# Retention projection of a hybrid diffusion layer: read-back rows in buffers of their own, and the first two output blocks taken by halves of the tokens

## The chip, the cores and the metric

The kernel runs on one core of one Trainium2 chip. The metric is device time in microseconds (us) of one execution; lower is better. The median of three runs of the kernel before is 1781.46 us (1779.99 to 1782.4).

## The reference

The kernel computes one transformer-like layer on 1024 latent tokens and 256 context tokens with 1024 channels, in float32. The part that matters here is the end of its first half:

```python
o_ret = _merge_heads(on) * jax.nn.silu(g)                      # gated retention, tokens x 1024
merged = sigmoid(gate_na) * (o_na @ w_proj_na) + sigmoid(gate_ret) * (o_ret @ w_proj_ret)
x = x + g1 * (merged @ w_out)
hx2 = modulate(rmsnorm(x, norm2_g), sh2, sc2)
x = x + g2 * conv_ffn(hx2, w_up, conv_w, conv_b, w_down)
```

`o_ret @ w_proj_ret` is the product of this case: 1024 tokens by 1024 channels by 1024 channels.

## The kernel before

Everything is held with channels on the 128 partitions and tokens along the free dimension. 1024 tokens are two halves of 512, 1024 channels are eight blocks of 128. A float32 operand is used as a pair: `split` makes a high part by a cast on ScalarE (ACT, line 86) and a low part by a subtraction on VectorE (DVE, line 87). A product is then three matmuls on TensorE (PE): high times high, high times low, low times high (lines 110, 111, 112). Each takes a 128x128 piece of weights and 512 tokens.

Weights arrive by `wload`: `rawload` (lines 89 to 92) brings 128x512 floats (256 KB) into a ring of three places (tag `raw`), and `split` turns them into a pair in a ring of six places (tag `wc`). All DMAs are issued by SyncE (SP) in one fixed order; an SP instruction that waits holds up all that stand behind it. The order on every engine is set at build time by a list scheduler from the order in which the code is written; `late` keeps an instruction at its place in the program's order.

The stages around the change, one after the other on PE:

1. **Gates.** Twelve-matmul steps of a seven-product scheme (`Gates`, rows `u` at L1374). Each step splits one weight pair. Units of the retention store their results, the gated retention rows, to DRAM (`d_orr`: eight channel blocks `k`, each 1024 tokens). Units of the merge, the last ones, store to `d_pn` and `d_gate` (rows `c` at L1482).
2. **Retention projection** (`pr`, lines 110 to 112). For each of eight output blocks `db` and each half of the tokens a chain of 24 matmuls: eight channel blocks `k`, three matmuls each, against the eight row pairs `orr[half, k]`. The first weights tile of a block serves `k` 0 to 3, the second 4 to 7. Then DVE multiplies the sum by its gate (`sg`, L1595), GpSimd (POOL) adds the other branch (L1596), and `split` makes `mh` and `ml`.
3. **Output projection** (`om`, lines 121 to 123), whose weights are `w_out`, with the second norm, and then the feed-forward half.

Before stage 2 the sixteen half rows `orr[half, k]` are read back from `d_orr` by `orr_raw`, which uses `rawload`, so the ring of three that the weights use. Those of half 0 are loaded during the last ten gate steps, one a step; those of half 1 in the loop at `db == 0`. The pairs `orr` lie where the normalised input `hx` lay: rows of half 1 with `k` 4 to 7 take the places that the very last gate step still reads.

Of the kernel before, what the change touches and what calls it, by code (L numbers as in the profile page):

```python
# [8 lines left out]
F32 = mybir.dt.float32  # L9
F32R = mybir.dt.float32r  # L10
AF = mybir.ActivationFunctionType
ALU = mybir.AluOpType
# [4 lines left out]
P = 128  # L17
D = 1024
KB = D // P
# [10 lines left out]
RH = 4  # L30
# [10 lines left out]
def tile_hybrid_layer(ctx, tc: tile.TileContext, io, dbg=None):  # L41
    nc = tc.nc
    vec, act, pool, pe, sync = nc.vector, nc.scalar, nc.gpsimd, nc.tensor, nc.sync

    def sb(name, side, bufs=1):
        return tc.alloc_tile_pool(name=name, bufs=bufs, side=side, reuse_waits="tile")
# [11 lines left out]
    d_orr = dram.tile([RH * 2, P, T], F32, name="d_orr")  # L58
# [24 lines left out]
    wpool = sb("wstream", "left")  # L83

    def split(hi, lo, src, lo_eng=None):
        act.copy(hi, src)  # L86
        (lo_eng or vec).tensor_tensor(lo, src, hi.bitcast(F32), ALU.subtract)  # L87

    def rawload(src, pin=lambda ins: ins):
        raw = wpool.tile([P, 512], F32, tag="raw", bufs=3, name="raw")  # L90
        pin(sync.dma_start(raw, src))
        return raw

    def wtile():
        return wpool.tile([P, 2, 512], F32R, tag="wc", bufs=6, name="wc")

    def wload(src, lo_eng=None, into=None):
        raw = rawload(src)
        wc = into if into is not None else wtile()
        split(wc[:, 0], wc[:, 1], raw, lo_eng)  # L100
        return wc

    def chain(out, wcs, hi, lo, step=24):
        n = 4 * len(wcs)
        for k in range(n):
            wc = wcs[k // 4]
            c0 = (k % 4) * P
            wh, wl = wc[:, 0, c0 : c0 + P], wc[:, 1, c0 : c0 + P]
            xh, xl = hi(k), lo(k)
            pe.matmul(out, wh, xh, start=k == 0, stop=False)  # L110
            pe.matmul(out, wh, xl, start=False, stop=False)  # L111
            pe.matmul(out, wl, xh, start=False, stop=k == n - 1)  # L112
            if (k + 1) % step == 0 and k + 1 < n:
                yield

    def mm_a(out, wcs, hi, lo):
        for _ in chain(out, wcs, hi, lo):
            pass
# [415 lines left out]
    late = tc.keep_in_program_order  # L534
# [703 lines left out]
    def down_sums(pool_, j0, j1, bufs=8):  # L1238
        def load(j, n):
            t = pool_.tile([P, 512], F32, tag="pj", bufs=bufs, name="pj")  # L1240
            sync.dma_start(t, io["w_down"][n % 2, NH * (n // 2) + j])
            return t

        ts, store = [load(j0, n) for n in range(4)], None
        yield
        for j in range(j0, j1):
            nxt = []
            for n, (c, x, y, o) in enumerate(((1, 1, 0, 0), (3, 3, 1, 1), (2, 3, 0, 3), (4, 2, 3, 2))):
                late(pool.tensor_tensor(ts[o], ts[x], ts[y], ALU.subtract))
                if store:  # L1250
                    sync.dma_start(*store)
                store = (d_w[j, c - 1], ts[o])
                if j + 1 < j1:
                    nxt.append(load(j + 1, n))
                yield
            ts = nxt
        sync.dma_start(*store)
# [71 lines left out]
    KH = KB // 2  # L1329

    def g_ps(name):
        return pg.tile([P, 512], F32, tag="g", bufs=6, name=name)

    def g_raw(name):
        return rr.tile([P, 512], F32, tag="r", bufs=10, name=name)
# [21 lines left out]
    for n in range(KB):  # L1357
        raw = g_raw("onr")
# [128 lines left out]
    for db in range(KB):  # L1487
# [3 lines left out]
        wp = [wload(io["w_pna"][db, 0])]  # L1491
        for half in range(2):
            sl_ = slice(half * 512, half * 512 + 512)
            m = g_ps("pn")
            mm_a(m, wp, lambda k: ona[0][:, k, sl_], lambda k: ona[1][:, k, sl_])
            t = onap.tile([P, 512], F32, tag="pn", bufs=3, name="pnt")
            if (db, 0) in spilled:
                g = onap.tile([P, 512], F32, tag="sg", bufs=2, name="sgt")
# [24 lines left out]

    orr = {}

    def orr_raw(half, k):
        i, kb = (k // KH if half else 1 - k // KH), k % KH + KH * half
        orr[half, k] = [hxpool.tile([P, 512], F32R, tag=f"{t}{i}{kb}", bufs=1, name="orr") for t in ("high", "low")]
        return orr[half, k], rawload(d_orr[k, :, half * 512 : half * 512 + 512], late)

    gate_sums = down_sums(gr, RET_SUMS, GATE_SUMS)
    steps = interleaved(0, len(gu))
    n0, fetched = steps.index((len(gu) - 1, 0)), None
    for n, (i, k) in enumerate(steps):
        gu[i].step(k)
        if n % 3 == 1:
            next(gate_sums, None)
        if fetched:
            split(*fetched[0], fetched[1])
            fetched = None  # L1540
        if n0 <= n < n0 + 2 * RH:
            fetched = orr_raw(0, n - n0)
    wp0 = [wload(io["w_pret"][0, i]) for i in range(2)]
    for _ in gate_sums:
        pass
    gr.release()
# [6 lines left out]
    def gtile(half, dt, name):  # L1553
        return gpool[half].tile([P, 512], dt, tag="g", bufs=2 * KB + 1, name=name)

    sg = {}

    def merge_load(db, halves=(0, 1)):
        for half in halves:
            sg[db, 0, half] = gtile(half, F32, "sg")  # L1560
            sync.dma_start(sg[db, 0, half], d_pn[db, half])
            sg[db, 1, half] = t = gtile(half, F32, "sg")
            sync.dma_start(t, d_gate[2 * db + 1, half])
            if (db, 1) in spilled:
                act.activation(t, t, AF.Sigmoid)
# [4 lines left out]
    def brow(i, t):  # L1570
        sync.dma_start(t, d_ada[8 * i : 8 * i + 8].rearrange("a b -> (a b)").unsqueeze(0).to_broadcast([P, D]))
        return t

    pjp = sb("out_sums", "right")
    out_sums = down_sums(pjp, GATE_SUMS, NH, 7)
    mg = {}
    wp_next = wp0
    for db in range(KB):
        wp = wp_next
        if db == 0:  # L1580
            merge_load(0, (0,))
            for k in range(2 * RH):
                hl, raw = orr_raw(1, k)
                split(*hl, raw)
            merge_load(0, (1,))
        if db + 1 < KB:
            wp_next = [wload(io["w_pret"][db + 1, i]) for i in range(2)]
            merge_load(db + 1)
        if db == 2:
            brow(0, gate1)  # L1590
        for half in range(2):
            m = g_ps("pr")
            mm_a(m, wp, lambda k: orr[half, k][0], lambda k: orr[half, k][1])
            g = sg[db, 1, half]
            vec.tensor_tensor(g, m, g, ALU.mult)  # L1595
            (vec if db == KB - 1 else pool).tensor_tensor(g, g, sg[db, 0, half], ALU.add)  # L1596
            h_, l_ = gtile(half, F32R, "mh"), gtile(half, F32R, "ml")
            split(h_, l_, g)
            mg[db, half] = (h_, l_)
            if db > 1:  # L1600
                next(out_sums, None)
    pjp.release()
    wo = {}
    for kb in range(KB):
# [450 lines left out]
def build(nc, arrays):  # L2055
    io = {k: nc.dram_tensor(f"in_{k}", a.shape, mybir.dt.from_np(a.dtype), kind="ExternalInput").ap() for k, a in arrays.items()}
    io["out"] = nc.dram_tensor("out_0_dram", (T, D), F32, kind="ExternalOutput").ap()
    with tile.TileContext(nc) as tc:
        tile_hybrid_layer(tc, io)
# [11 lines left out]
```

## Time and profile before

| | before |
|---|---|
| median of three runs | 1781.46 us (1779.99 to 1782.4) |
| the profiled execution | 1783.34 us, span 1781.6 us |
| PE busy | 1728.4 us, 97% of the span |
| DVE, ACT, POOL busy | 73%, 48%, 32% |
| mean granted clock of PE | 0.988 |
| gates stage ends, retention projection begins to end | 929.0, 931.3 to 1027.6 us |

Times inside the span are us from its start. PE is busy nearly all the time, so a change of the time has to come from stretches in which PE waits or runs at a lower granted clock. A matmul row shows 0.39 us, but matmuls overlap: at full pace one starts every 0.227 us.

### The profile page before, as it was taken

What the parts mean: (1) busy time and instruction counts of PE and PEld (TensorE: products, weight loads), DVE (VectorE), ACT (ScalarE), POOL (GpSimd) and SP (SyncE); (2) the same over time, 40 slices, a digit from 0 to 9 for tenths busy, and PEclk for the clock granted to TensorE, in tenths of its full rate; (3) what the DMA queues carried; (4) which work ended last, traced back from release to release, by engine and by line L of the source; (5) the groups of instructions that cost most, each with busy time, mean ns of one, the idle gap of its engine ahead of it and who ended that gap; (6) DMA issues with size and microseconds to landing.
All of it is one profiled execution on the core that took longest, in us unless ns stands there. A gap on an engine that the chain in (4) does not pass through costs nothing.

```text
span 1781.6 us, 24740 instructions
## 1 busy us (share of the span) xinstructions
PE 1728.4 (97%) x8357; PEld 1431.6 (80%) x8357; DVE 1309.0 (73%) x2458; ACT 850.2 (48%) x1833; POOL 569.1 (32%) x477
## 2 busy tenths in 40 slices
PE   8799999999999999999999999989999999999997
PEld 3588888888888888778877888868888888788886
DVE  5878888765776766777655556879989989875755
ACT  5667666652443434443444333544444444554444
POOL 2610000002334343554412400065555555211444
PEclk9899999999999999999999999999999999999999
DMA  9133334432231212677558633642332332586754
GB/s 344 57 116 119 113 111 137 140 112 101 70 107 48 72 39 71 205 234 252 177 178 277 224 140 138 238 137 89 107 101 89 108 118 101 165 285 195 241 160 160
DMA packets 139552, 261.62 MB, mean 147 GB/s; under 512 B 15872, under 2 KB 28320, under 8 KB 139424
## 3 DMA queue, kind: packets, MB, share of 16 engines
q1 hardware_dynamic: 139424, 260.03, 43.6%
q8 instruction: 66, 1.08, 0.3%
q14 instruction: 62, 0.51, 0.1%
HBM read 187.87 MB, written 69.48 MB: 144 GB/s over the span
## 4 chain that ended last, share of the span: by engine, by line
PE 41%; issue 6%; DVE 4%; POOL 3%; DMA 2%; ACT 1%; SPq 0%; POOLq 0%; ACTq 0%; DVEq 0%
PE u L1374 28%; PE y L1374 4%; PE pr L110 2%; PE pr L111 2%; PE pr L112 2%; PE om L121 1%; PE om L122 1%; PE om L123 1%; DVE wc L87 1%; POOL x L1885 1%; DMA ur<-in_w_up 0%; DVE v L1662 0%; DMA raw<-d_orr 0%; DVE b L1350 0%; POOL pd L1922 0%
## 5 line engine op out<-in xcount | busy, mean ns | idle before, releaser
L1374 PE MATMUL u<-T,wc 128*128 128x512 f32 x960 | 227.9, 393 | 6.4 <-ACT pu L1408 5.8
L1374 PEld LDWEIGHTS u<-T,wc 128*128 128x128 f32 x960 | 180.9, 189 | 47.6 <-ACT pu L1408 9.1
L1374 PE MATMUL y<-wc,ahl 128*128 128x512 f32 x924 | 210.7, 390 | 3.3 <-DVE wc L87 1.8
L1374 PEld LDWEIGHTS y<-wc,ahl 128*128 128x128 f32 x924 | 173.4, 188 | 40.3 <-DVE wc L87 2.5
L87 DVE TENSOR_TENSOR wc<-ur,wc 128x512 fp32r<-128x512 f32 x137 | 125.3, 917 | 65.2 <-ACT wc L86 65.1
L86 ACT CAST wc<-ur 128x512 fp32r<-128x512 f32 x137 | 85.1, 622 | 129.9 <-PE y L1374 72.1
L111 PE MATMUL mm<-low,wc 128*128 128x512 f32 (+1 forms) x328 | 124.1, 378 | 0.0
L1374 PE MATMUL u<-h2a,wc 128*128 128x512 f32 x480 | 112.3, 390 | 0.7 <-DVE pu L1417 0.7
L110 PE MATMUL mm<-hx,wc 128*128 128x512 f32 x264 | 107.5, 407 | 0.3 <-DVE vc L221 0.3
L1374 PEld LDWEIGHTS u<-h2a,wc 128*128 128x128 f32 x480 | 90.1, 188 | 19.8 <-DVE pu L1417 1.2
L112 PE MATMUL mm<-hx,wc 128*128 128x512 f32 x264 | 105.2, 399 | 0.0
L86 ACT CAST wc<-s 128x512 fp32r<-128x512 f32 x80 | 49.7, 622 | 91.5 <-PE u L1374 86.9
L123 PE MATMUL mm<-wc,low 128*128 128x512 f32 (+1 forms) x240 | 91.3, 380 | 0.0
L1508 POOL TENSOR_TENSOR col<-col,bcol 128x32 f32<-128x32 f32 x1 | 0.3, 253 | 281.5 <-DVE aw L538 281.5
L1374 PE MATMUL u<-hxT,wc 128*128 128x512 f32 x384 | 89.6, 389 | 0.0
L87 DVE TENSOR_TENSOR wc<-s,wc 128x512 fp32r<-128x512 f32 x80 | 86.4, 1082 | 2.4 <-ACT wc L86 2.0
L1374 PEld LDWEIGHTS u<-hxT,wc 128*128 128x128 f32 x384 | 72.1, 188 | 14.9
L87 DVE TENSOR_TENSOR wc<-raw,wc 128x512 fp32r<-128x512 f32 x92 | 69.5, 763 | 18.2 <-ACT wc L86 18.1
L1383 POOL TENSOR_TENSOR s<-ur 128x512 f32<-128x512 f32 x20 | 36.7, 1835 | 125.1 <-DVE wc L87 71.7
L121 PE MATMUL mm<-wc,hx 128*128 128x512 f32 x192 | 75.3, 392 | 0.6 <-ACT r L1105 0.6
L122 PE MATMUL mm<-wc,hx 128*128 128x512 f32 x192 | 75.3, 392 | 0.0
L86 ACT CAST wc<-raw 128x512 fp32r<-128x512 f32 x92 | 56.7, 621 | 32.0 <-DMA raw<-in_w_pret 5.3
(393 smaller groups left out, 4722.7 us busy)
## 6 DMA issues: line engine op xcount, KB each, us to landing
ur<-in_w_up SPq DMA_DIRECT2D x80, 256.0 KB, 3.0
ur<-d_a SPq DMA_DIRECT2D x77, 256.0 KB, 3.1
aw<-in_w_ada SPq DMA_DIRECT2D x32, 512.0 KB, 3.2
pj<-in_w_down SPq DMA_DIRECT2D x44, 256.0 KB, 4.8
d_w<-pj SPq DMA_DIRECT2D x44, 256.0 KB, 2.0
d_a<-sa SPq DMA_DIRECT2D x44, 256.0 KB, 2.0
ur<-d_w SPq DMA_DIRECT2D x44, 256.0 KB, 3.7
d_a<-at SPq DMA_DIRECT2D x33, 256.0 KB, 2.7
```

The source lines that it names most:

```text
L86: act.copy(hi, src)
L87: (lo_eng or vec).tensor_tensor(lo, src, hi.bitcast(F32), ALU.subtract)
L110: pe.matmul(out, wh, xh, start=k == 0, stop=False)
L111: pe.matmul(out, wh, xl, start=False, stop=False)
L112: pe.matmul(out, wl, xh, start=False, stop=k == n - 1)
L121: pe.matmul(out, ah, bh, start=first, stop=False)
L122: pe.matmul(out, ah, bl, start=False, stop=False)
L123: pe.matmul(out, al, bh, start=False, stop=last)
L1374: pe.matmul(out, a, b, start=first and n == 0, stop=last and n == 2, skip_group_check=True)
L1383: pool.tensor_tensor(self.s1, self.a21, self.a22, ALU.add)
L1508: pool.tensor_tensor(col[:, 16:48], col[:, 16:48], bcol[:, 16:48], ALU.add)
L1885: pool.tensor_tensor(z, z, fg[:, gs(dh)], ALU.mult)
```

## The change

The rows `orr` are loaded and split by two functions instead of one, and the place that they are loaded into is given by the caller. Half 0's first four rows still use the ring of three, but five to two steps before the last gate unit begins; its other four go into places of the gates' own raw weights (`orw` from `g_raw`), one to four steps after that unit has begun. The eight rows of half 1 go into eight of the seventeen places of that half's pool (`gtile(1, F32, "orw")`), so none of them takes a place of the ring, and all eight loads are written ahead of all eight splits. Output blocks 0 and 1 are taken by halves: both blocks' half 0, then both blocks' half 1. Blocks 2 to 7 go as before. Weights of block 1 are written ahead of block 0's products.

```diff
-    def orr_raw(half, k):
+    def orr_load(raw, half, k, pin=late):
+        pin(sync.dma_start(raw, d_orr[k, :, half * 512 : half * 512 + 512]))
+        return half, k, raw
+
+    def orr_split(half, k, raw):
         i, kb = (k // KH if half else 1 - k // KH), k % KH + KH * half
         orr[half, k] = [hxpool.tile([P, 512], F32R, tag=f"{t}{i}{kb}", bufs=1, name="orr") for t in ("high", "low")]
-        return orr[half, k], rawload(d_orr[k, :, half * 512 : half * 512 + 512], late)
+        split(*orr[half, k], raw)
...
-        if n0 <= n < n0 + 2 * RH:
-            fetched = orr_raw(0, n - n0)
-    wp0 = [wload(io["w_pret"][0, i]) for i in range(2)]
+        if n0 - KH - 1 <= n < n0 - 1:
+            fetched = orr_load(wpool.tile([P, 512], F32, tag="raw", bufs=3, name="raw"), 0, n - n0 + KH + 1)
+        elif n0 < n <= n0 + KH:
+            fetched = orr_load(g_raw("orw"), 0, n - n0 - 1 + KH)
...
+    merge_load(0, (0,))
+    rows = [orr_load(gtile(1, F32, "orw"), 1, k, lambda ins: ins) for k in range(2 * RH)]
+    for r in rows:
+        orr_split(*r)
+    wp[1] = pret_load(1)
+    merge_load(1, (0,))
+    for half in range(2):
+        if half:
+            merge_load(0, (1,))
+            merge_load(1, (1,))
+        for db in range(2):
+            pret(db, half)
+    for db in range(2, KB):
+        wp[db] = pret_load(db)
+        merge_load(db)
...
         for half in range(2):
-            m = g_ps("pr")
-            mm_a(m, wp, lambda k: orr[half, k][0], lambda k: orr[half, k][1])
...
+            pret(db, half)
+            next(out_sums, None)
```

(`pret` holds the lines that the loop held, `pret_load` the two `wload`s of a block.)

The instructions are the same in number and kind on every engine; only their order changes, and it changes only between the gates' last unit but one and the middle of the retention projection. On POOL the order is the same throughout.

First place, SP's queue in the last gate steps. In both, `raw_10243` and `raw_10248` are block 0's weights; the rows `raw` or `orw` from `d_orr` are half 0's; `c` are the gates' results. Before:

```order
L91 DMA raw_10144<-d_orr_63 128x512
L91 DMA raw_10171<-d_orr_63 128x512
L1474 DMA o_10221<-d_pn_62 128x512
L1482 DMA d_gate_61<-c_10162 128x512
L1482 DMA d_pn_62<-c_10190 128x512
L91 DMA raw_10198<-d_orr_63 128x512
L91 DMA raw_10243<-in_w_pret 128x512
L1482 DMA d_gate_61<-c_10215 128x512
L91 DMA raw_10248<-in_w_pret 128x512
```

After, where `raw_10322` is the first weights tile of block 1:

```order
L91 DMA raw_10243<-in_w_pret 128x512
L1482 DMA d_gate_61<-c_9993 128x512
L91 DMA raw_10248<-in_w_pret 128x512
L91 DMA raw_10322<-in_w_pret 128x512
L1482 DMA d_pn_62<-c_10058 128x512
L1527 DMA orw_10062<-d_orr_63 128x512
L1527 DMA orw_10084<-d_orr_63 128x512
L1527 DMA orw_10111<-d_orr_63 128x512
L1527 DMA orw_10132<-d_orr_63 128x512
L1474 DMA o_10181<-d_pn_62 128x512
```

Block 0's weights stood behind half 0's last row; now they stand ahead of its last four rows, six gate results earlier, and block 1's first tile with them.

Second place, SP's queue where half 1's rows stand. `c_10217` and `c_10238` are the last two results of the gates. Before:

```order
L91 DMA raw_10276<-d_orr_63 128x512
L1482 DMA d_pn_62<-c_10238 128x512
L91 DMA raw_10282<-d_orr_63 128x512
L91 DMA raw_10288<-d_orr_63 128x512
L1561 DMA sg_10322<-d_pn_62 128x512
L91 DMA raw_10294<-d_orr_63 128x512
L1563 DMA sg_10324<-d_gate_61 128x512
L91 DMA raw_10300<-d_orr_63 128x512
L1561 DMA sg_10337<-d_pn_62 128x512
L91 DMA raw_10306<-d_orr_63 128x512
```

After:

```order
L91 DMA raw_10565<-in_w_pret 128x512
L1571 DMA sg_10269<-d_pn_62 128x512
L1573 DMA sg_10271<-d_gate_61 128x512
L1482 DMA d_gate_61<-c_10217 128x512
L1527 DMA orw_10274<-d_orr_63 128x512
L1527 DMA orw_10276<-d_orr_63 128x512
L1527 DMA orw_10278<-d_orr_63 128x512
L1527 DMA orw_10280<-d_orr_63 128x512
L1482 DMA d_pn_62<-c_10238 128x512
L1527 DMA orw_10282<-d_orr_63 128x512
L1527 DMA orw_10284<-d_orr_63 128x512
L1527 DMA orw_10286<-d_orr_63 128x512
```

Four of half 1's rows now stand ahead of the last gate result's store and four right behind it, with no other load in between; `raw_10565`, ahead of them, is already the first tile of block 3's weights.

Third place, PE at the end of block 0's first chain (`pr_10347`, after: `pr_10337`). Before:

```order
L111 MATMUL pr_10347<-orr_10197,wc_10250 128x512
L112 MATMUL pr_10347<-orr_10196,wc_10250 128x512
L110 MATMUL pr_10378<-orr_10274,wc_10245 128x512
L111 MATMUL pr_10378<-orr_10275,wc_10245 128x512
L112 MATMUL pr_10378<-orr_10274,wc_10245 128x512
L110 MATMUL pr_10378<-orr_10280,wc_10245 128x512
```

After:

```order
L111 MATMUL pr_10337<-orr_10157,wc_10250 128x512
L112 MATMUL pr_10337<-orr_10156,wc_10250 128x512
L110 MATMUL pr_10368<-orr_9920,wc_10324 128x512
L111 MATMUL pr_10368<-orr_9921,wc_10324 128x512
L112 MATMUL pr_10368<-orr_9920,wc_10324 128x512
L110 MATMUL pr_10368<-orr_9943,wc_10324 128x512
```

The second chain read half 1's rows (`orr_10274`) with block 0's weights; now it reads half 0's rows again (`orr_9920`) with block 1's weights (`wc_10324`), and half 1's rows are first read by the third chain.

More of the change, by code (lines that the diff above doesn't have):

```diff
@@ L1538, in tile_hybrid_layer, with pret_load @@
         if fetched:
-            split(*fetched[0], fetched[1])
+            orr_split(*fetched)
             fetched = None
-        if n0 <= n < n0 + 2 * RH:
-            fetched = orr_raw(0, n - n0)
-    wp0 = [wload(io["w_pret"][0, i]) for i in range(2)]
+        if n0 - KH - 1 <= n < n0 - 1:
+            fetched = orr_load(wpool.tile([P, 512], F32, tag="raw", bufs=3, name="raw"), 0, n - n0 + KH + 1)
+        elif n0 < n <= n0 + KH:
+            fetched = orr_load(g_raw("orw"), 0, n - n0 - 1 + KH)
+    def pret_load(db):
+        return [wload(io["w_pret"][db, i]) for i in range(2)]
+    wp = {0: pret_load(0)}
     for _ in gate_sums:
@@ L1576, in tile_hybrid_layer, with pret @@
     mg = {}
[L1577 to L1584, printed above, removed]
-            merge_load(0, (1,))
-        if db + 1 < KB:
-            wp_next = [wload(io["w_pret"][db + 1, i]) for i in range(2)]
-            merge_load(db + 1)
+    def pret(db, half):
+        m = g_ps("pr")
+        mm_a(m, wp[db], lambda k: orr[half, k][0], lambda k: orr[half, k][1])
+        g = sg[db, 1, half]
+        vec.tensor_tensor(g, m, g, ALU.mult)
+        (vec if db == KB - 1 else pool).tensor_tensor(g, g, sg[db, 0, half], ALU.add)
+        h_, l_ = gtile(half, F32R, "mh"), gtile(half, F32R, "ml")
+        split(h_, l_, g)
+        mg[db, half] = (h_, l_)
+    merge_load(0, (0,))
[6 more added lines that the diff above has]
+        if half:
+            merge_load(0, (1,))
+            merge_load(1, (1,))
[4 more added lines that the diff above has]
+        merge_load(db)
         if db == 2:
@@ L1591, in tile_hybrid_layer @@
         for half in range(2):
-            m = g_ps("pr")
-            mm_a(m, wp, lambda k: orr[half, k][0], lambda k: orr[half, k][1])
[L1594 to L1601, printed above, removed]
+            pret(db, half)
+            next(out_sums, None)
     pjp.release()
```

## Prediction

> **What bounds the kernel now.** The page's busy times come first, then the chain that ended last.
>
> ```profile
> PE 1728.4 (97%) x8357; PEld 1431.6 (80%) x8357; DVE 1309.0 (73%) x2458; ACT 850.2 (48%) x1833; POOL 569.1 (32%) x477
> PE u L1374 28%; PE y L1374 4%; PE pr L110 2%; PE pr L111 2%; PE pr L112 2%; PE om L121 1%; PE om L122 1%; PE om L123 1%; DVE wc L87 1%; POOL x L1885 1%; DMA ur<-in_w_up 0%; DVE v L1662 0%; DMA raw<-d_orr 0%; DVE b L1350 0%; POOL pd L1922 0%
> ```
>
> PE bounds the whole; what the change can win lies where PE isn't busy near its stage. `raw<-d_orr` stands on the chain. So next the stretches around the stage, by engine: last gate steps, the projection's start, its rest, the output projection.
>
> ```profile
> core 0: us, PE busy (x) PEld busy (x) DVE busy (x) ACT busy (x) POOL busy (x), PEclk, DMA share, GB/s
> 902.00:929.00 27.00, 27.00 (x120) 22.16 (x118) 14.53 (x22) 11.08 (x19) 0.00 (x0) 1.00 0.49 172
> 929.00:957.80 28.80, 23.76 (x77) 16.58 (x77) 16.39 (x22) 14.97 (x25) 3.26 (x2) 0.82 0.83 272
> 957.80:1027.60 69.80, 69.80 (x309) 57.83 (x308) 35.61 (x52) 23.49 (x41) 27.49 (x20) 1.00 0.71 236
> 1027.60:1130.00 102.40, 102.40 (x479) 85.00 (x479) 69.80 (x178) 35.98 (x79) 4.69 (x8) 1.00 0.44 160
> ```
>
> Ahead of 929.0 and from 957.8 on PE is full at clock 1.00; only 929.0 to 957.8 has gaps, and a clock of 0.82. The rest of the projection gives the full pace: 69.80 us for 308 matmuls (one row counts twice at the border), 0.2266 us each. All 384 matmuls would take 87.0 us; they take 929.0 to 1027.6, so 98.6. **11.6 us are lost there**, and this is the most that the change can win. The gaps one by one, in order of time on PE:
>
> ```profile
> 928.78 0.39 PE L1374 MATMUL u<-hx,wc 128*128 128x512 f32 x1
> 931.27 0.51 PE L110 MATMUL pr<-orr,wc 128*128 128x512 f32 x1 [2.10 <-ACT wc L86]
> 941.95 0.50 PE L111 MATMUL pr<-orr,wc 128*128 128x512 f32 x1 [0.72 <-DVE orr L87]
> 944.12 0.50 PE L110 MATMUL pr<-orr,wc 128*128 128x512 f32 x1 [0.54 <-ACT orr L86]
> 944.84 0.50 PE L111 MATMUL pr<-orr,wc 128*128 128x512 f32 x1 [0.22 <-DVE orr L87]
> 947.03 0.79 PE L110 MATMUL pr<-orr,wc 128*128 128x512 f32 x1 [1.45 <-ACT orr L86]
> ```
>
> Idle: 2.10 + 0.72 + 0.54 + 0.22 + 1.45 = 5.03 us. The first gap waits for block 0's weights, the others for half 1's rows. The granted clock in the same stretch:
>
> ```profile
> 931.30:935.00 3.70, 3.70 (x10) 2.65 (x11) 1.94 (x3) 2.16 (x4) 0.00 (x0) 0.65 0.91 312
> 935.00:936.00 1.00, 1.00 (x5) 0.77 (x4) 0.69 (x1) 0.15 (x1) 0.00 (x0) 0.60 0.93 268
> 941.00:947.00 6.00, 3.09 (x10) 1.27 (x8) 2.88 (x4) 2.40 (x5) 0.34 (x1) 0.92 0.81 253
> 947.00:953.40 6.40, 6.37 (x15) 4.41 (x16) 4.36 (x5) 3.07 (x6) 1.65 (x1) 0.54 0.77 246
> 953.40:957.60 4.20, 4.20 (x21) 3.42 (x19) 2.10 (x4) 3.17 (x7) 0.00 (x0) 1.00 0.89 303
> ```
>
> Clock loss is length times what is missing: 3.70 x 0.35 + 1.00 x 0.40 + 6.00 x 0.08 + 6.40 x 0.46 = 5.1 us. It follows the gaps and ends by itself. The remaining 1.5 us are the five restarts: a gap is counted from the end of a 0.39 us row, though the next matmul could start 0.23 us after its start (0.16 each, 0.8), and rows that trickle in. Last, what the gaps wait for: SP's queue, and the split behind the longest wait.
>
> ```profile
> 926.16 0.43 SPq L91 DMA_DIRECT2D raw<-d_orr  x1
> 926.70 0.39 SPq L91 DMA_DIRECT2D raw<-in_w_pret  x1
> 927.87 0.32 SPq L1482 DMA_DIRECT2D d_gate<-c  x1
> 930.71 0.32 SPq L91 DMA_DIRECT2D raw<-d_orr  x1
> 932.57 0.32 SPq L1482 DMA_DIRECT2D d_pn<-c  x1
> 942.82 0.37 SPq L91 DMA_DIRECT2D raw<-d_orr  x1
> SPq L91 <- DVE orr L87: 8.4, 8, 1.4
> 946.36 0.62 ACT L86 CAST orr<-raw 128x512 fp32r<-128x512 f32 x1 [2.30 <-DMA raw<-d_orr]
> ```
>
> Block 0's weights are issued at 926.70, behind half 0's last row (926.16). Half 1's eight rows are issued from 930.71 to 942.82, because SP waits 8.4 us in eight places for a subtraction that frees a place of the ring; the last is split at 946.36, and PE's last gap ends with it.
>
> **The change, part by part.** No instruction is added or removed; every term is a move.
>
> *Half 0's rows and block 0's weights.* The weights' loads move six gate results up SP's queue, ahead of 926.70 by more than 15 us. What then sets the split is a place among the six pairs: one gate step is 12 x 0.2266 = 2.72 us, and block 0's first tile follows the tenth of the last ten steps, so it takes the pair of the step five before the last, free at 929.0 - 5 x 2.72 = 915.4; the next three tiles follow at 918.1, 920.8 and 923.6. Splitting takes a cast and a subtraction:
>
> ```profile
> L86 ACT CAST orr<-raw x16: 615/620/624, 881.3 to 947.7; 128x512 fp32r<-128x512 f32 x16
> L87 DVE TENSOR_TENSOR orr<-raw,orr x16: 682/693/1778, 881.9 to 948.3; 128x512 fp32r<-128x512 f32 x16
> 909.17 1.39 SPq L91 DMA_DIRECT2D raw<-d_orr  x3
> ```
>
> That is 1.3 us, so block 0 is ready by about 920 and block 1 by 926. Half 0's last four rows are issued at the place that 909.17 shows. The first gap (2.10) goes. The price is on DVE and ACT, which take some six more splits before 929.0: 4.1 and 3.7 us against 12 and 16 idle us in the row 902.00:929.00; cover is ample.
>
> *SP waits for ring places* at block 1's second tile and at blocks 2 and 3, each until a subtraction paced by PE's gate steps. Behind them stand the gates' stores and `o` loads, on which only the gates' last multiplications wait, not PE. Cost 0; if that cover went, the last store (932.57) and with it four rows would come later, which the next part prices.
>
> *Half 1's rows.* The ring's 8.4 us of waits go. Rows 0 to 3 stand behind the store at 927.87 and are issued at 928.3 to 930. Rows 4 to 7 stand behind the gates' last store (932.57), whose sigmoid now has a cast of block 2's weights and another sigmoid ahead of it on ACT, at most the two (0.62 each by the cast row above, so 1.2) and at least nothing, as ACT may do them while it waits; I take the nearer to the middle, half a microsecond: issued 933.3 to 935. How long a row takes is bounded by the 256 KB loads of the trace:
>
> ```profile
> raw<-d_orr SPq DMA_DIRECT2D x16, 256.0 KB, 3.5
> o<-d_pn SPq DMA_DIRECT2D x8, 256.0 KB, 2.9
> raw<-in_w_up SPq DMA_DIRECT2D x8, 256.0 KB, 5.1
> 951.10 1.65 POOL L1596 TENSOR_TENSOR sg<-sg 128x512 f32<-128x512 f32 x1 [9.75 <-DVE sg L1595]
> ```
>
> I take 3.5, the same tensor: the last row lands at 938.5. By 2.9 it is 937.9, by 5.1 it is 940.1. Its cast stands behind `mh` of block 0's half 0, which waits for POOL's 1.65 us after the first chain (934.4, so 937.3): no delay. With two casts and a subtraction the row is ready at 940.4 (942 by the long landing).
>
> *Blocks 0 and 1 by halves.* PE goes on at 929.0; two chains of half 0 take 2 x 24 x 0.2266 = 10.9 us, so half 1's first row is wanted at 939.9 and each further one 0.68 later: the fifth at 942.6, the last at 944.7. The fifth lands at 936.8 and is ready at 938.1. Margin 4.3 us, or 2.7 by the long landing. All gaps at rows go. Were the rows' loads alone moved and the chains' order kept, half 1's rows would be wanted 5.4 us earlier, the fifth at 937.2 and the last at 939.2, and miss by about 1 us; the halves are what hides them.
>
> *What comes late next.* Block 2's chains begin at 950.8, block 3's at 961.7. Block 3's second tile stands behind the rows and some fourteen 256 KB loads and one of 512 KB. Rates in the stage:
>
> ```profile
> 929.00:940.00 11.00, 8.90 (x31) 6.78 (x31) 5.84 (x9) 5.87 (x10) 0.26 (x1) 0.84 0.86 289
> 950.00:960.00 10.00, 10.00 (x39) 7.88 (x38) 6.42 (x9) 5.32 (x9) 3.31 (x2) 0.86 0.91 290
> 960.00:970.00 10.00, 10.00 (x46) 8.29 (x45) 4.59 (x7) 3.75 (x6) 2.54 (x3) 1.00 1.03 374
> PE u L1374 <- ACT pu L1408: 5.8, 2, 5.6
> ```
>
> At 289 GB/s a load of 0.262 MB takes 0.9 us, twenty of them from 932 end at 950: 14 us to spare before 964.4. Behind the stage PE's longest wait (5.6 us, fence's last row) is for ACT's own result much later, not for a transfer; it moves along.
>
> [...] In the trace a gap of 2.10 us is followed by a clock of 0.65, and gaps of 0.2 to 1.45 us within 941 to 947 by 0.54. [...]
>
> **Sum.** 11.6 us of loss minus 0 left over: the profiled execution (1783.34) would come to 1771.7. It lies 1.9 above the median of the runs (1781.46), so the median comes to 1769.9, told as 1770.
>
> **The rivals.**
>
> 1. *Half 1's rows come a little late.* For it: they share the DMA engines with thirteen transfers (3.4 MB) from 926.4 on, at 0.86 share already in the row 929.00:940.00; against it: 3.4 MB at 289 GB/s end at 938.2, before 939.9. A microsecond of gap has cost 11.6 / 5.03 = 2.3 us here. A gap of 2 us costs 4.6: 1774.5.
> 2. *The low clock doesn't come from the gaps.* Then only idle and restarts go, 6.5 us: 1775.0. Against it: clock 1.00 in the stretches without gaps.
> 3. *No gain: output projection's weights stay where they are.* Their loads stand behind POOL's subtractions in SP's queue. If these kept their times, PE would give the 11.6 back at 1016: 1781. Against it: POOL's order is unchanged and each of its adds waits for a chain of PE, so it moves along.
> 4. *Slower: transfers become the bound.* From 929.0 to the stage's end 28.8 x 272 + 69.8 x 236 = 24300 GB/s x us, or 24.3 MB, were moved; five weight tiles now come earlier (1.3), leaving 23.0 MB for 87.0 us: 264 GB/s. If the engines sustained under 23.0 / 98.6 = 233 GB/s, the gain would be gone; at 220 the stage takes 104.5 us, 5.9 more: 1787. For it: 236 in the row of the stage's rest; against it: a share of 0.71 there, and 374 in the row 960.00:970.00.
>
> The named change is only half done, as half 0's first four rows keep the ring; they are split by about 907, so this costs nothing.
>
> **How the numbers follow.** Forecast 0.82, rival 1 0.08, rival 2 0.03, rival 3 0.04, rival 4 0.03. A difference of 0.2% (3.6 us) is about what a measurement can tell from none. Faster: 0.82 + 0.08 + 0.03, less 0.01 for later rows: 0.92; same 0.05; slower 0.03. The range begins at the lowest run less 11.6, 1768.4, so 1768; it reaches over rivals 1 and 2 with the spread of the runs (0.9 above the median), 1776.
>
> **What would show it.** Right: PE without gaps from the last `u` to the last `pr`, clock 1.00 throughout, block 0's weights cast by about 916 to 919, half 1's last row cast before 941, the output projection starting near 1016. Wrong: a gap at the third chain (rows), at the seventh (block 3's weights), or low clock without a gap. Wrong in size: a new gap in the output projection.

## The result, and the profile after

The changed kernel takes 1771.87 us in the median (1770.56 to 1775.67) against 1781.93 us for the kernel before on the same chip: a ratio of 0.9939, 95% interval 0.9926 to 0.9953. The forecast was 1770.0. Timed once more in a later session it took 1770.89 us (1768.48 to 1773.55) against 1783.83, ratio 0.9927 (0.9911 to 0.9944). The profiled execution of after is 1775.67 us, span 1773.9 us.

The stretches around the stage, in the columns of the prediction's second fence; its gates end 2.2 us later than in the profile of before:

```profile
902.00:929.00 27.00, 27.00 (x121) 22.36 (x120) 18.16 (x30) 13.33 (x25) 0.00 (x0) 1.00 0.61 186
929.00:957.80 28.80, 28.80 (x129) 23.85 (x128) 15.91 (x24) 14.75 (x25) 5.17 (x4) 1.00 0.93 323
957.80:1016.00 58.20, 58.20 (x259) 48.18 (x258) 31.30 (x45) 19.88 (x36) 24.46 (x18) 1.00 0.74 242
1016.00:1120.00 104.00, 104.00 (x487) 86.28 (x486) 69.84 (x176) 36.70 (x80) 4.70 (x8) 1.00 0.44 155
```

In the row 929.00:957.80 PE was busy 23.76 us at a clock of 0.82; now it is busy all 28.80 us at 1.00, with 129 matmuls in it instead of 77. The ends of the stage on PE: the gates' last matmul, the projection's first one, the output projection's first one.

```profile
930.96 0.39 PE L1374 MATMUL u<-hx,wc 128*128 128x512 f32 x1
931.18 0.39 PE L110 MATMUL pr<-orr,wc 128*128 128x512 f32 x1
1018.22 0.39 PE L121 MATMUL om<-wo,mh 128*128 128x512 f32 x1
```

The projection follows the gates without a gap, and its 384 matmuls take 1018.22 - 931.18 = 87.0 us, which is 384 x 0.2266. Of the 11.6 us lost before, nothing is left. Below, "stage loss" means the time from the end of the gates (start of the last `u` plus 0.23) to the first `om`, less 87.0.

### The profile page after: what moved, and what is told of

It reads as the page before. It is cut to its first block, busy times and chain, and to the rows that moved or that the text cites. A ratio compares the mean times of both kernels' runs of the same rounds, so it can differ in the third digit from the quotient of the medians.

```text
span 1773.9 us, 24736 instructions
## 1 busy us (share of the span) xinstructions
PE 1727.6 (97%) x8357; PEld 1432.2 (81%) x8357; DVE 1306.4 (74%) x2458; ACT 849.6 (48%) x1833; POOL 567.2 (32%) x477
## 4 chain that ended last, share of the span: by engine, by line
PE 42%; issue 6%; DVE 4%; POOL 3%; DMA 2%; ACT 1%; SPq 0%; POOLq 0%; ACTq 0%; DVEq 0%
PE u L1374 29%; PE y L1374 4%; PE pr L112 2%; PE pr L111 2%; PE pr L110 2%; PE om L122 1%; PE om L123 1%; PE om L121 1%; DVE wc L87 1%; DMA vo<-d_h 1%; POOL x L1902 1%; DVE b L1350 0%; POOL pd L1939 0%; DVE hxT L87 0%; POOL x L1947 0%
```

## The experiments

Theory: PE meets a row of waits, and only the one that it meets next counts. Each of the change's three parts (half 0's rows and block 0's weights earlier; half 1's rows in places of their own; blocks 0 and 1 by halves) takes one of them away and lays the next one open; the low clock is the consequence of the gaps. Rivals: each part is worth its own gap, so that the parts add up; or the low clock has another cause.

Differences are the ratio less one, times the median of before in the same session (1783.83, 1783.47 for the pairs and the first run with a made gap, 1785.68 for the halves with the weights ahead), with the 95% interval; the -2.1, -3.6 and +4.5 us that later expectations name for the parts are differences of medians. The idle time and the stage loss are those of one profiled execution. "A" is half 0's part, "B" half 1's places, "C" the halves.

| parts in the kernel | ratio (95%) | us against before | PE idle in the stage | stage loss |
|---|---|---|---|---|
| none (before) | 1 | 0 | 5.03 | 11.6 |
| A | 0.9986 (0.9974 to 0.9998) | -2.5 | 3.68 | 8.3 |
| B | 0.9977 (0.9964 to 0.9991) | -4.1 | 5.57 | 10.0 |
| C, block 1's weights behind the rows | 1.0029 (1.0017 to 1.0041) | +5.2 | 12.99 | 17.0 |
| C, block 1's weights ahead of them | 0.9961 (0.9947 to 0.9976) | -7.0 | 3.39 | 6.7 |
| A and B | 0.9965 (0.9952 to 0.9978) | -6.2 | 1.36 | 2.8 |
| B and C, weights behind the rows | 1.0004 (0.9991 to 1.0018) | +0.7 | 8.30 | 13.2 |
| A and C, weights ahead of the rows | 0.9963 (0.9949 to 0.9976) | -6.6 | 2.55 | 6.3 |
| A, B and C (the change) | 0.9927 (0.9911 to 0.9944) | -13.0 | 0 | 0.0 |

### The change once more

> The changed kernel once more, for the size of the gain. The two-waits theory (the gain is the 11.6 us that PE lost between the gates and the middle of the projection, and nothing else) says 9 to 12 us faster than before, and a projection of 87.0 us from its first product to the first of the output projection. A rival, that part of the gain is taken back for good by something later, says 10 us or less in every run and a stretch behind the projection that is longer than before in each profile.

No gap and no loss in the stage: -13.0 us (-15.9 to -10.0), which holds the 11.6; the first measurement of the same program gave -10.9 (0.9939 of 1781.93). Of the rival's two signs the first didn't come, the second did: behind the stage the two profiles of the change take 755.7 and 755.9 us, that of before 754.0. Over all fourteen profiles of this text that stretch takes 751.8 to 758.8 us, and 752.6 in the last experiment's kernel, which has the change too; so it isn't a price of the change.

### Half 0's part alone

Half 1's rows take the ring again, and blocks 0 and 1 go in the order of before:

```diff
-    rows = [orr_load(gtile(1, F32, "orw"), 1, k, lambda ins: ins) for k in range(2 * RH)]
-    for r in rows:
-        orr_split(*r)
+    for k in range(2 * RH):
+        orr_split(*orr_load(wpool.tile([P, 512], F32, tag="raw", bufs=3, name="raw"), 1, k))
```

> Only the first part of the change: half 0's rows earlier and in the gates' places, so block 0's weights early; half 1's rows through the ring of three as before, and no halves. Additive theory: the first gap and its clock go (2.1 + 1.7 + 0.3), 4.1 us faster, the later gaps stay at 2.9 us. Two-waits theory: the first gap goes, but half 1's rows are wanted 4 us earlier and still come through the ring, so the gaps at them grow to 5 or more us; 1 to 4 us faster.

The first gap is gone and the rest is still there. PE's waits in the stage, by what it waited for (us in total, times, longest):

```profile
PE pr L110 <- ACT orr L86: 2.0, 3, 1.2
PE pr L111 <- DVE orr L87: 0.8, 4, 0.2
PE pr L110 <- ACT wc L86: 0.8, 1, 0.8
```

PE begins its second chain 5.67 us after the gates' last matmul instead of 9.93, so it also asks for half 1's rows earlier. These come earlier too, though less: the last one is ready 17.5 us after that matmul instead of 20.2. The idle time at the rows is 2.87 us, against 2.93 before: the two-waits theory's 5 us or more didn't come, the additive theory's 2.9 did. The second chain takes 12.5 us instead of 11.4, and 0.81 us of waiting for block 1's second weights tile are new. Of the 4.3 us won at the first chain 3.3 are left at the end of the stage. The time, 2.5 us faster (0.4 to 4.6), fits the 1 to 4 us of the one theory and the 4.1 of the other, so this run doesn't decide between them.

### Half 1's places alone

```diff
-        if n0 - KH - 1 <= n < n0 - 1:
-            fetched = orr_load(wpool.tile([P, 512], F32, tag="raw", bufs=3, name="raw"), 0, n - n0 + KH + 1)
-        elif n0 < n <= n0 + KH:
-            fetched = orr_load(g_raw("orw"), 0, n - n0 - 1 + KH)
+        if n0 <= n < n0 + 2 * RH:
+            fetched = orr_load(wpool.tile([P, 512], F32, tag="raw", bufs=3, name="raw"), 0, n - n0)
```

(and the chains as before)

> Only the second part: half 1's rows in eight places of their own; half 0's rows and block 0's weights as before, and no halves. Additive and two-waits theory agree here: the first gap (2.1 us) and its clock stay, the gaps at half 1's rows go, 6 to 7.5 us faster. A rival, that the order by halves is what closes those gaps, says they stay at 2 us or more: at most 4 us faster.

```profile
PE pr L110 <- ACT wc L86: 2.6, 1, 2.6
PE pr L112 <- DVE wc L87: 2.2, 1, 2.2
PE pr L111 <- DVE orr L87: 0.8, 1, 0.8
```

The expected gain of 6 to 7.5 us was missed: 4.1 (1.6 to 6.4). Of the 2.93 us at the rows 0.75 are left, so the rival's 2 us or more at them is wrong, though its "at most 4 us faster" fits the time. A wait of 2.2 us for weights that wasn't there before has come in their place, in the third chain: block 1's weights stand on SP behind the rows, as they did before, and PE now gets to them 17.0 us after the gates' last matmul instead of 21.3. This agrees with the theory that a wait taken away lays the next one open; my count of the waits was short by one.

### The halves alone, in two forms

```diff
+    wp[1] = pret_load(1)          # second form only
     merge_load(0, (0,))
-    rows = [orr_load(gtile(1, F32, "orw"), 1, k, lambda ins: ins) for k in range(2 * RH)]
-    for r in rows:
-        orr_split(*r)
-    wp[1] = pret_load(1)
+    for k in range(2 * RH):
+        orr_split(*orr_load(wpool.tile([P, 512], F32, tag="raw", bufs=3, name="raw"), 1, k))
+    wp[1] = pret_load(1)          # first form only
```

(half 0's rows and block 0's weights as before)

> Only the third part: blocks 0 and 1 by halves of the tokens; all rows through the ring as before. Block 1's weights then stand behind half 1's eight rows in the ring and are wanted one chain earlier. Two-waits theory: PE waits some 9 to 10 us for them after its first chain, 4 to 9 us slower than before. Additive theory: the halves alone hide half 1's rows, up to 7.5 us faster.

> As the run with the halves alone (which came 4.5 us slower, by a gap of 10.55 us for block 1's weights), but with block 1's weights written ahead of half 1's eight rows; rows still through the ring, half 0's rows and block 0's weights at the times of before. If the weights' place behind the ring's rows made the halves alone slow: the gap of 10.55 us goes; the first gap of 2.1 to 2.9 us with its one stretch of half clock stays (4 to 4.5 us), and the rows, behind two more loads in the ring, leave gaps of 0 to 2.5 us: stage loss 4 to 10 us, so 1.5 to 7.5 us faster than before (ratio 0.996 to 0.999). If the halves themselves cost (the order of chains or its later use of the rows): 2 us or more slower again (above 1.001).

The waits of the first form, and where block 1's weights stand in its SP queue:

```profile
PE pr L110 <- ACT wc L86: 13.0, 2, 10.6
```

```profile
942.04 0.32 SPq L1527 DMA_DIRECT2D raw<-d_orr  x1
942.94 2.14 SPq L91 DMA_DIRECT2D raw<-in_w_pret  x2
```

By halves, PE wants block 1's weights right after its first chain; they are issued at 942.94, behind the eighth row, which had to wait for a place of the ring. PE stands still for 10.55 us. With the same two loads ahead of the rows:

```profile
PE pr L110 <- ACT wc L86: 2.4, 1, 2.4
PE pr L110 <- ACT orr L86: 0.8, 1, 0.8
PE pr L111 <- DVE orr L87: 0.2, 1, 0.2
```

The long wait is gone, and 5.2 us slower turn into 7.0 us faster. So it wasn't the order of the chains that made the first form slow, but the place of two loads in the queue. What these loads ahead of the rows would be worth without the halves wasn't run.

### Two parts at a time

A and B: the changed kernel with the chains in the order of before.

```diff
-    for half in range(2):
-        if half:
-            merge_load(0, (1,))
-            merge_load(1, (1,))
-        for db in range(2):
-            pret(db, half)
-    for db in range(2, KB):
+    merge_load(0, (1,))
+    for db in range(KB):
```

> Half 0's rows and block 0's weights early and half 1's rows in places of their own, but the chains in the order of before. Theory of the chain of waits (each wait uncovers the next, and only what PE reaches last counts): no gap at the first chain; half 1's rows come at their times of the changed kernel, the last ready about 14 us after the last gate matmul, while the old order of chains wants it 10.2 us after it; gaps of 2 to 4 us at rows 4 to 7 plus low clock behind them: stage loss 5 to 8 us, 4 to 6.5 us faster than before (ratio 0.9963 to 0.9978). The on-record estimate 'miss by about 1 us' would give a loss of 2.3 us, 9 us faster (0.995). Theory that the two parts add (measured alone -2.1 and -3.6 us): 5.7 us faster; theory that the moved loads are all that counts: 11 to 12 us faster (0.9935).

```profile
PE pr L111 <- DVE orr L87: 0.8, 2, 0.6
PE pr L110 <- ACT orr L86: 0.5, 1, 0.5
```

In this execution half 1's rows miss by 1.36 us in three gaps, and the clock stays at 1.00, so 2.8 us are lost. The gaps of 2 to 4 us and the loss of 5 to 8 that the theory expected were too large; the estimate on record (a miss of about 1 us, a loss of 2.3) was near. By the ratio the kernel is 6.2 us faster (3.9 to 8.6), which fits the theory's 4 to 6.5 and the additive 5.7 alike, and is less than the 8.8 us that this profile's stage gives. The halves are thus worth 2.8 us in the profiled executions and 6.8 by the ratios (4.7 with the change's first measurement), which come from two chips; the difference stays open.

B and C: half 0's lines as in "half 1's places alone", the rest as in the changed kernel.

> Half 1's rows in places of their own and the two blocks by halves, but half 0's rows and block 0's weights at the times of before. Chain of waits: the first gap of 2.1 to 2.6 us for block 0's weights stays with its low clock; block 1's weights stand behind the eight rows on SP and are wanted after the first chain, about 939, and come at 940 to 943, a second gap of 1 to 4 us: stage loss 6 to 11 us, 1 to 6 us faster than before (ratio 0.9966 to 0.9995). If the parts added (-3.6 and +4.5 alone): 0.9 us slower. If half 0's part were only worth its own gap (2.1 us idle and its clock): 6 to 7 us faster.

```profile
PE pr L110 <- ACT wc L86: 8.1, 2, 5.3
```

```profile
932.60 3.29 SPq L1527 DMA_DIRECT2D orw<-d_orr  x7
935.99 1.25 SPq L91 DMA_DIRECT2D raw<-in_w_pret  x2
```

A first gap of 2.86 us, then 5.26 us for block 1's weights, issued behind the eight rows (the last seven in this fence): longer than the 1 to 4 us expected, since issuing them ended at 937.24 and PE could go on at 943.77 only. The stage loses 13.2 us instead of the 6 to 11 expected, and there is no gain (-1.6 to +3.2 us) instead of one of 1 to 6; the additive theory's 0.9 us slower fits the time. In the change these weights are ahead of the rows only because half 0's part moved everything in front of them.

A and C: block 1's weights ahead, half 1's rows through the ring.

```diff
-    rows = [orr_load(gtile(1, F32, "orw"), 1, k, lambda ins: ins) for k in range(2 * RH)]
-    for r in rows:
-        orr_split(*r)
     wp[1] = pret_load(1)
+    merge_load(0, (0,))
+    for k in range(2 * RH):
+        orr_split(*orr_load(wpool.tile([P, 512], F32, tag="raw", bufs=3, name="raw"), 1, k))
```

> Half 0's rows and block 0's weights early, block 1's weights ahead of half 1's rows, and the two blocks by halves, but half 1's rows through the ring of three. Chain of waits: no first gap; SP waits for a split at every ring place as before, so rows 4 to 7 come 15 to 17 us after the last gate matmul, wanted 13.6 to 15.7 us after it: gaps of 0 to 2 us, stage loss 0 to 4.5 us, 7 to 11.6 us faster than before (ratio 0.9935 to 0.996). Theory that places of their own are what hides the rows: the ring's 8.4 us of waits stay, and it is no more than 4 us faster (0.9978 or above). If the parts added (-2.1 and +4.5): 2.4 us slower.

```profile
PE pr L110 <- ACT orr L86: 1.3, 1, 1.3
PE pr L111 <- DVE orr L87: 1.2, 2, 1.0
```

Gaps of 2.55 us at the rows, over the 0 to 2 expected, and 6.3 us lost, over the 0 to 4.5, again with a low clock (0.54):

```profile
945.00:950.00 5.00, 3.79 (x9) 2.46 (x9) 4.03 (x5) 3.12 (x6) 1.27 (x1) 0.54 0.90 286
```

It is 6.6 us faster (4.3 to 9.1), under the 7 to 11.6 expected and over the other theory's 4. So the halves don't hide rows that wait for the ring: places of their own take away the last 6.3 us of loss (6.6 us against 13.0 by the ratios, on two chips).

Do the parts add? By the times that hangs on C's form. With the first, which is how the change writes it, A, B and C sum to -2.5 - 4.1 + 5.2 = -1.4 us, where all three together give -13.0. With the second they sum to -13.6, and none of the pairs differs from its sum by more than the intervals either. So what the times show beyond the noise is one dependence: C gains only where block 1's weights stand ahead of the rows, and in the change it is A that brings them there. The idle time in the stage shows more. A takes away 1.35 us of it, B adds 0.54, C in its second form takes away 1.64, in sum 2.45; all three together take away 5.03, and A and B together 3.67 instead of 0.81. In what PE waits for, the parts don't add.

### Made gaps

Half 0's first row is read back last of its eight, and its low part is made on POOL, three, two or one times over (the result is the same), so that PE waits at the projection's second matmul and nowhere near it.

```diff
-        split(*orr[half, k], raw)
+        hi, lo = orr[half, k]
+        act.copy(hi, raw)
+        for _ in range(3 if (half, k) == (0, 0) else 1):     # 3, 2 or 1
+            (pool if (half, k) == (0, 0) else vec).tensor_tensor(lo, raw, hi.bitcast(F32), ALU.subtract)
```

> The changed kernel with the first row of half 0 read back last of its eight and its low part made three times over on POOL, so that PE waits at the second matmul of the retention projection for an estimated 1 to 2 us and nowhere else near it. Theory that any such gap starts a stretch of low clock: the granted clock falls to about 0.5 for some 3.4 us behind it, the stage loses gap plus 1.7 us, about 3 us in all. [...]

> The same with the low part made twice: a gap of 3.96 - 1.37 = 2.6 us. Theory that a microsecond of gap costs 2.3 us: loss 6.0 us. Theory that a gap costs itself plus a stretch of low clock: 2.8 us with the clock at 1.00, 4.5 us with one stretch, 6.2 us with two. [...]

> As the run with a gap of 3.96 us, but the low part of the row that comes last is made once on POOL instead of three times: the gap at the second matmul of the projection is 3.96 - 2 x 1.37 = 1.2 us. Theory that a microsecond of gap costs 2.3 us: loss 2.8 us. Theory that a gap costs itself plus a stretch of low clock of its own length (about 3.4 us at half clock, 1.7 us), when it costs clock at all: loss 1.4 us with the clock at 1.00, or 3.1 to 4.8 us with one or two such stretches. [...]

Three times over, the gap and the six us behind it:

```profile
930.73 0.79 PE L111 MATMUL pr<-orr,wc 128*128 128x512 f32 x1 [3.96 <-POOL orr L1536]
930.73:936.73 6.00, 6.00 (x14) 4.73 (x15) 2.39 (x5) 2.61 (x5) 0.00 (x0) 0.51 1.02 353
936.73:942.00 5.27, 5.27 (x25) 4.32 (x24) 3.63 (x6) 2.38 (x4) 1.66 (x1) 1.00 1.06 398
```

Twice over:

```profile
933.07 0.50 PE L111 MATMUL pr<-orr,wc 128*128 128x512 f32 x1 [1.15 <-POOL orr L1536]
933.07:942.00 8.93, 8.93 (x39) 7.38 (x40) 4.37 (x8) 3.73 (x7) 0.00 (x0) 1.00 0.92 312
```

The gaps came out otherwise than planned, 3.96, 1.15 and none, because the row's cast stood 0.8, 2.0 and 3.5 us ahead of the gates' last matmul. The gap of 3.96 us cost 7.0: itself and 6.00 x 0.49 = 2.9 us of clock (and -7.7 us against before, so some 5 us slower than the change). The gap of 1.15 cost 1.5: itself and its restart, at clock 1.00. Once over, there was no gap and no loss. At 2.3 us lost per us of gap they would have cost 9.1 and 2.6. The low clock is thus a consequence of a gap, as a gap made on purpose brings it, in a place where the clock was 1.00; but it isn't in proportion to it. No made gap lies between 1.15 and 3.96 us; for those stand the first gaps of the runs above (last section). The kernels with the low part made twice and once ran one time each, in 1780.72 and 1770.84 us, where before took 1782.21. Of the 9.9 us between them only 1.5 lie in the stage: the first one's gates end 5.0 us later (931.31 against 926.28), and behind the stage it takes 3.3 us longer. So these two times say nothing of the gap; its price is read from the stage.

### The last gate's sigmoid without another sigmoid ahead of it

```diff
-    merge_load(0, (0,))
     rows = [orr_load(gtile(1, F32, "orw"), 1, k, lambda ins: ins) for k in range(2 * RH)]
     for r in rows:
         orr_split(*r)
+    merge_load(0, (0,))
```

> The changed kernel with the loads and sigmoids of block 0's first gates written behind half 1's rows, so that the last gate's sigmoid stands ahead of them on ScalarE and no instruction that waits for a transfer is ahead of it. Theory that half 1's late rows come from the sigmoid of sg that waits for its own transfer (2.29 us): the last gate's store is issued some 1.6 us sooner after the last gate matmul (5.9 us instead of 7.5), the last row is cast at least 1 us sooner after it (13 us instead of 15), and the time stays, as nothing waits for the rows: no gap on PE in the projection, loss 0, time 1768 to 1775. Theory that the rows come late by the transfers' own pace (323 GB/s at a share of 0.93): the store moves and the last row comes no sooner than 14.5 us. Rival on the other side: block 0's gates now come late for the first multiplication by them, the sums' places stay full, and PE waits at the third or fourth chain for 1 us or more.

The baselines in that expectation (7.5 and 15 us) were worked out wrongly, with the gates' end of before; in the changed kernel's own profile they are 936.25 - 930.96 = 5.3 us and 943.89 - 930.96 = 12.9 us. On ACT and SP, with the gates' last matmul at 928.25:

```profile
930.70 0.62 ACT L86 CAST orr<-orw 128x512 fp32r<-128x512 f32 x1 [3.38 <-DMA orw<-d_orr]
931.75 0.63 ACT L1479 ACTIVATE c<-c 128x512 f32<-128x512 f32 x1
938.98 0.62 ACT L86 CAST orr<-orw 128x512 fp32r<-128x512 f32 x1 [0.62 <-DMA orw<-d_orr]
```

```profile
933.28 0.32 SPq L1482 DMA_DIRECT2D d_pn<-c  x1
933.64 2.35 SPq L1527 DMA_DIRECT2D orw<-d_orr  x2
```

The sigmoid of `sg` is gone from ahead of the last one, but a row's cast that waits for its own transfer took its place: the store is only 0.3 us sooner (5.0). Half the expectation failed. The last row's cast is 938.98 - 928.25 = 10.7 us after the gates' end all the same, 2.2 us sooner, since only two rows are left to be issued behind the store instead of four and `sg`'s two loads no longer go ahead of the rows. PE shows no gap, the stage loss is 0, and the one execution took 1769.93 us: the rows' time isn't what PE waits for.

## Why the prediction was right, point by point

- **The term of 11.6 us** came out whole: 0.0 left in both profiles of the change. In its make-up the clock was counted 0.5 us too high: of the half clock behind the rows' gaps 0.98 us lie in the last gap, from 946.05 to 947.03, where PE stood idle. So it is 5.03 us of idle time, 4.6 of clock and 2.0 of restarts; the total is the same.
- **Half 0's rows and block 0's weights.** Two weight tiles cast in one go, forecast for 916 to 919 at the gates' end of before; less the 2.2 us, 918.4:

```profile
920.61 1.14 ACT L86 CAST wc<-raw 128x512 fp32r<-128x512 f32 x2
```

- **SP at ring places.** In the stretch 900 to 960 its waits for the rows' subtractions fell from 9.7 us to 1.3; of the prediction's 8.4, which are those from 926 to 958, none is left. Its waits for the weights' places cost PE nothing, as forecast.

```profile
SPq L91 <- DVE orr L87: 1.3, 1, 1.3
SPq L91 <- DVE wc L87: 5.2, 7, 1.7
```

- **Half 1's rows: the mis-sized step.** Rows 0 to 3 are issued from 930.50, so 928.3 on the scale of before, as forecast. For rows 4 to 7 I had half a microsecond for the cast and the sigmoid ahead of the last gate's sigmoid, bounds 0 to 1.2. SP and ACT show this:

```profile
930.50 2.46 SPq L1527 DMA_DIRECT2D orw<-d_orr  x4
936.25 0.32 SPq L1482 DMA_DIRECT2D d_pn<-c  x1
936.61 2.63 SPq L1527 DMA_DIRECT2D orw<-d_orr  x4
```

```profile
934.34 0.63 ACT L1575 ACTIVATE sg<-sg 128x512 f32<-128x512 f32 x1 [2.29 <-DMA sg<-d_gate]
934.88 0.62 ACT L1479 ACTIVATE c<-c 128x512 f32<-128x512 f32 x1
943.89 0.62 ACT L86 CAST orr<-orw 128x512 fp32r<-128x512 f32 x1 [0.88 <-DMA orw<-d_orr]
```

The sigmoid ahead is that of `sg`, and it waits 2.29 us for its own load. The last gate's sigmoid so starts 3.9 us after the gates' last matmul (934.88 - 930.96), where it was 2.3 before (931.12 - 928.78): 1.6 us, outside my bounds, which priced the instruction and not the transfer that it waits for. Issuing the four rows then took 2.63 us instead of the 1.7 that I had, and the last one was cast 4.65 us after its issue ended, not 3.5. It is ready (cast and subtraction, 1.3) at 945.2, on the scale of before 943.0, and was wanted at 944.7: a margin of 1.7 us where I had 4.3. One of the signs of being right failed with it: the last row's cast starts at 943.89, 941.7 on the scale of before, and not before 941. The time stayed only because the margin was larger than the error.
- **The halves.** "Miss by about 1 us" without them: 1.36 us of gaps.
- **What comes late next, and the third and fourth rivals.** Nothing did. The output projection began at 1018.22, on the scale of before 1016.0, and PE was busy throughout the row 1016.00:1120.00, so the third rival, which had its weights come as late as before, is out. Transfers ran at 323 GB/s in the stage's first 28.8 us, well above the 233 below which the gain would have gone.
- **The first rival's price** (2.3 us lost per us of gap) was wrong, as the made gaps show; the second rival is refuted by them.
- **The sum.** 1770.0 against 1771.87 and 1770.89, inside the spread of the runs. The profiled execution gained 7.7 us, not 11.6: its gates ended 2.2 us later, and it lost 1.7 us more behind the stage. The first isn't the change's, as the second profile of the same program ends the gates at 928.67, 0.1 us from before. Of the second, 1.3 us (1.6 in the second profile) lie at one place near the end, where PE ran the same 59 matmuls at a lower clock than in before (last section).

## What to carry to other kernels

Price a gap of PE by what it would uncover, not by its length: write down for each load when it is wanted after the edit, and look at what stands behind it in its queue; here three parts of -2.5, -4.1 and +5.2 us made -13.0 together, and the third alone was worth -7.0 once two loads stood elsewhere in the queue. When an instruction moves ahead of another on the same engine, the price of the move is what it waits for, not how long it runs (here the sigmoid of `sg` waited 2.29 us and ran 0.63). Where several small edits each seem worth little, try them together before dropping them.

## What the hardware showed that I had not expected

**The loss of clock didn't follow the length of the gap.** The first gaps of before and of four other runs were 2.10, 2.61 (B), 2.44 and 2.40 (C in its two forms) and 2.86 us (B and C); the five us from the restart, in before:

```profile
931.27:936.27 5.00, 5.00 (x14) 3.68 (x15) 2.66 (x4) 2.35 (x4) 0.00 (x0) 0.66 0.91 302
```

All five have a clock of 0.66 there (0.68 for the gap of 2.40), so each lost 5 x 0.34 = 1.7 us (1.6), with gaps from 2.10 to 2.86 us; the gap of 1.15 us lost nothing, that of 3.96 us 2.9. In before the clock of 0.50 lasts 3.41 us behind the first gap, which is worth 1.7 us, and 6.83 us at the rows' gaps:

```profile
932.40:935.81 3.41, 3.41 (x10) 2.65 (x9) 1.46 (x3) 1.37 (x3) 0.00 (x0) 0.50 0.91 294
946.05:952.88 6.83, 5.85 (x13) 3.97 (x14) 3.94 (x5) 3.19 (x6) 1.65 (x1) 0.50 0.80 264
```

**The same 59 matmuls took three different times.** Near the end of every one of these kernels PE waits twice for a weight pair and then runs the same 59 matmuls. Here are these in before (behind waits of 1.55 and 1.39 us), in the second profile of the change (0.80 and 1.38), and in A and B (1.16 and 1.39):

```profile
1760.04 13.68 PE L1374 MATMUL y<-wc,ahl 128*128 128x512 f32 x59 [1.39 <-DVE wc L87]
```

```profile
1748.69 15.26 PE L1374 MATMUL y<-wc,ahl 128*128 128x512 f32 x59 [1.38 <-DVE wc L87]
```

```profile
1750.12 16.52 PE L1374 MATMUL y<-wc,ahl 128*128 128x512 f32 x59 [1.39 <-DVE wc L87]
```

The 59 matmuls took 13.65 to 13.68 us in six of the fourteen profiles, 14.98 to 15.27 in six, and 16.52 and 16.55 in two; longer gaps didn't go with longer times (the longest, 1.84 and 1.39, gave 13.67 in one run and 15.25 in another). The granted clock went with the times. These are stretches of 3.41 us at the same place, in the same three executions, in the columns of the prediction's second fence (PE's busy time first, the clock third from the end):

```profile
1755.01:1758.42 3.41, 1.86 (x9) 1.17 (x7) 1.52 (x2) 2.57 (x5) 1.77 (x5) 1.00 0.53 197
1758.42:1761.84 3.42, 2.03 (x9) 1.50 (x9) 3.21 (x6) 3.21 (x6) 0.18 (x1) 1.00 0.71 264
```

```profile
1745.60:1749.01 3.41, 1.24 (x4) 0.48 (x3) 1.80 (x4) 2.89 (x8) 0.81 (x2) 1.00 0.78 291
1749.01:1752.42 3.41, 3.41 (x9) 2.63 (x8) 3.41 (x7) 2.62 (x6) 0.00 (x0) 0.50 0.38 142
```

```profile
1746.02:1749.43 3.41, 1.55 (x6) 0.75 (x4) 1.47 (x3) 2.56 (x6) 1.11 (x3) 1.00 0.81 302
1749.43:1752.85 3.42, 2.73 (x7) 2.15 (x8) 3.42 (x7) 3.42 (x8) 0.00 (x0) 0.50 0.43 161
1752.85:1756.26 3.41, 3.41 (x10) 2.63 (x8) 1.43 (x3) 0.21 (x1) 0.00 (x0) 0.50 0.00 0
```

In before PE is busy for 1.86 and 2.03 us of two such stretches, and the clock of both is 1.00, as it is in the 13.68 us of the matmuls. In the second profile of the change PE is busy for 1.24 us of the first stretch, and the next is at 0.50; in A and B it is busy for 1.55 us, and the next two are at 0.50. In the retention projection of A the four waits of 1.25, 0.22, 0.20 and 0.22 us between 933.4 and 937.1 went with a loss (0.94 over 930 to 958, 28 x 0.06 = 1.7 us), while the three gaps of A and B, 1.36 us together, and the made gap of 1.15 us had a clock of 1.00 behind them. So waits of 2.94 us in sum (before) cost no clock, and waits of 2.18 (the second profile of the change) and 1.89 (A) did; what decides was not shown.

Two profiles can thus differ by 2.9 us at this place alone (13.65 and 16.55), so a change of this size is read from its own stage.
